# Head sums of an RWKV-7 block as single full-precision products, and third buffers for three evacuation tiles

## The chip, the cores and the metric

The kernel runs on one core of one Trainium2 chip. The metric is the device time of one execution in microseconds (us); the kernel before took 1866.65 us, the median of three runs (1861.1 to 1870.76 us). PE is TensorE, DVE is VectorE, ACT is ScalarE, POOL is GpSimd, SP is SyncE, which only issues DMAs here.

## What is computed

One layer of a decoder with two parallel branches, for a prompt of 1024 tokens and 8 samples of 8 tokens (1088 columns in all). Branch A is sliding-window attention; branch B is RWKV-7 time mixing, with 16 heads of 64 channels. The change touches branch B alone. What bears on it, from the reference:

```
kk = k * k_k.reshape(B_HEADS, HEAD_DIM)
kk = kk / jnp.maximum(jnp.sqrt(jnp.sum(kk * kk, axis=-1, keepdims=True)), 1e-12)
...
y, wkv_T = wkv_scan(r, decay, k, v, -kk, kk * a, wkv0)
mean = jnp.mean(y, axis=-1, keepdims=True)
var = jnp.mean(jnp.square(y - mean), axis=-1, keepdims=True)
y = (y - mean) * lax.rsqrt(var + GN_EPS) * lnx_g + lnx_b
y = y + jnp.sum(r * k * r_k, axis=-1, keepdims=True) * v
```

There are four sums over a head's 64 channels: the norm of the key (kk * kk), the mean of y, its variance, and the bonus (r * k * r_k).

## The kernel before

Channels lie on the 128 partitions (two heads to a tile), tokens on the free axis. The 8 tiles of two heads are worked through in pairs (p = 0 to 3), and each in four quarters of 256 tokens (the fourth has 320, the samples with it): 16 steps s of two tiles each, so 32 quarters in all.

**Dense projections.** All weight products are `d` tiles: operands are split into a high and a low part of type float32r (`whi`, `wlo`, `hhi`, `hlo`), and three products of 8 instructions each make one chunk of 364 or 360 columns (`mm3`, L183). Each chunk is evacuated by ACT, POOL and DVE. For a token-shifted projection (`shift_tile`, L391), ACT writes `pad` and `zz` (L404 to L406), POOL adds them (L407), and the result goes to DRAM. The tiles `pad` and `zz` have two buffers each, which gates (`gevac`), other projections (`spill`), `lora` and the raw low-rank weights (L655) share.

**The recurrence.** For each step s, `prefetch` (L643) loads a quarter from DRAM and squares the key into `kkn` on ACT (L663); `quarter` (L670) makes decay and key norm; `scores`, `invert` and `merge` build a small inverse, in which DVE runs 15 dependent pairs of tiny operations (L854, L856); `chain` (L921) carries the state through four chunks of 64 tokens, each with three rounds of PE product and DVE copy (`xs` L954, `vsu` L959, `vsu` L970); `post` (L1022) does the normalisation of y.

**The four sums.** Each is a product with a constant 128x128 matrix: `bone` (ones within a head) or `cen` (identity less the mean). The operand is first split by `split` (L232): ACT copies it to a float32r tile `shi` (L235), DVE subtracts that from the original into `slo` (L236); each of the two tags has one buffer in a pool. `sum2` (L239) then adds the two products in PSUM. The results are named `kn` (key norm, L694), `bo` (bonus, L745), `gc` (centring, L1029) and `gv` (variance, L1035); the halves are `shik`/`slok`, `shib`/`slob`, `shic`/`sloc`, `shiv`/`slov`. With 32 quarters there are 128 sums.

**The order.** On PE the order of the recurrence and the dense stream is written by the program: generators yield at points where they must wait, and `drive` (L142) picks the next by a planned clock. That clock is advanced by `mm` (L111) by a cost of each product:

```
self.clk += 0.024 if rhs.shape[0] == 32 else max(n / 2190, 0.085) if rhs.dtype == F32R else n / 1200 if transpose else max(n / 580, 0.066)
```

The other engines' orders are made by the framework's scheduler, by priorities. All engines take their instructions strictly in order. After the recurrence come the attention (`attention`) and the last projections (`final`), which the change does not touch.

Of the kernel before, what the change touches and what calls it, by code (L numbers as in the profile page):

```python
# [81 lines left out]
class Prog:  # L82
# [148 lines left out]

    def split(self, pool, src, n, nm):  # L232
        hi = pool.tile([P, 320], F32R, tag="shi", name=f"shi{nm}", bufs=1)[:, :n]
        lo = pool.tile([P, 320], F32R, tag="slo", name=f"slo{nm}", bufs=1)[:, :n]
        self.nc.scalar.activation(hi, src, AF.Copy)  # L235
        self.nc.vector.tensor_tensor(lo, src, hi.bitcast(F32), ALU.subtract)  # L236
        return hi, lo

    def sum2(self, ps, w, parts):  # L239

        self.mm(ps, w, parts[0], start=True, stop=False)
        self.mm(ps, w, parts[1], start=False, stop=True)


# [37 lines left out]
    def start(self, xp, w0):  # L282
# [7 lines left out]
        self.rco = ep.tile([P, NCONST - C_MI], F32, name="rco")  # L290
        self.bone = ep.tile([P, P], F32R, name="bone")
        self.cen = ep.tile([P, P], F32R, name="cen")
        bc = xp.tile([P, 2, P], F32, name="bc")
        for t, i in ((self.con, self.I["con"][:, :C_MI]), (prm, self.I["par"]), (self.rco, self.I["con"][:, C_MI:]),
# [89 lines left out]
        go(tk)  # L384
        nc.gpsimd.tensor_copy(self.bone, bc[:, 0, :])
        nc.gpsimd.tensor_copy(self.cen, bc[:, 1, :])
        nc.gpsimd.dma_start(self.O["ck"], self.I["ckn"][:, NS:, :])
# [3 lines left out]
    def shift_tile(self, idx, ti, out):  # L391

        nc, ep = self.nc, self.ep
        mu, om = self.par(Q_MU + ti), self.prd[:, ti:ti + 1]
        prev = [None]

        def evac(c0, c1, ps):
            m = min(c1, SEQ) - c0
            pad = ep.tile([P, 369], F32, tag="pad", name=f"pad{ti}_{c0}", bufs=2)
            z = ep.tile([P, 364], F32, tag="zz", name=f"zz{ti}_{c0}", bufs=2)  # L400
            if prev[0] is None:
                nc.vector.memset(pad[:, 0:1], 0.0)
# [28 lines left out]
    def gate(self, g):  # L431
        nc, ep = self.nc, self.ep

        def gevac(c0, c1, ps):
            t = ep.tile([P, 364], F32, tag="zz", name=f"gz{g}_{c0}", bufs=2)[:, :c1 - c0]
            x = ep.tile([P, 369], F32, tag="pad", name=f"gx{g}_{c0}", bufs=2)[:, :c1 - c0]
            nc.scalar.activation(x, ps, AF.Copy)
            self.sig_neg(t, t, x, -1.0, 0.0)
            nc.gpsimd.tensor_tensor(t, x, t, ALU.mult)
            nc.gpsimd.dma_start(self.d_g[g][:, c0:c1], t)  # L440
            self.mark(f"g{g}_{c0}")
        yield from self.dense(T_RKVG + 4 * g + 3, self.hhi, self.hlo, gevac)

    def spill(self, idx, dst, kind="copy", scale=1.0):
# [3 lines left out]
        def evac(c0, c1, ps):  # L448
            t = ep.tile([P, 364], F32, tag="zz", name=f"sp{idx}_{c0}", bufs=2)[:, :c1 - c0]
            if kind == "copy":  # L450
                nc.scalar.activation(t, ps, AF.Copy, scale=scale)
            else:
                x = ps
                if kind == "silu":
                    x = ep.tile([P, 369], F32, tag="pad", name=f"sx{idx}_{c0}", bufs=2)[:, :c1 - c0]
                    nc.scalar.activation(x, ps, AF.Copy)
# [186 lines left out]
    def prefetch(self, g, q):  # L643
# [10 lines left out]
        else:  # L654
            raw = ep.tile([P, 364], F32, tag="zz", name=f"w2r{nm}", bufs=2)[:, :2 * P]  # L655
            nc.sync.dma_start(raw, self.I["lora"][:, g].rearrange("p j c -> p (j c)"))
# [4 lines left out]
        nc.sync.dma_start(zk[:, :n], self.d_z[g][1][:, 256 * q:256 * q + n])  # L661
        kkn = ep.tile([P, 320], F32, tag="kkn", name=f"kkn_{nm}", bufs=2)
        nc.scalar.activation(kkn[:, :n], zk[:, :n], AF.Square, scale=self.par(Q_KK + g))  # L663
        parts = self.split(ep, kkn[:, :n], n, f"k{nm}")
        zr = ep.tile([P, 320], F32, tag="zr", name=f"zr_{nm}", bufs=2)
        nc.sync.dma_start(zr[:, :n], self.d_z[g][0][:, 256 * q:256 * q + n])
        self.mark(f"pf{nm}")
        return w2, zk, kkn, parts, zr

    def quarter(self, g, q, gi, f, pre):  # L670
# [8 lines left out]

        w2, zk, kkn, parts, zr = pre  # L680
        yield f"pf{g}_{q}", WD + 4.0 * gi, "m"
# [11 lines left out]
        pk = self.ps("a", f"kn{nm}", 2)  # L693
        self.sum2(pk[:, :n], self.bone, parts)  # L694
        if gi == 0:
# [43 lines left out]
    def bonus(self, g, q, S):  # L739
        nc, ep = self.nc, self.ep  # L740
        n, a0, zk, zv = 320 if q == 3 else 256, 256 * q, S["zk"], S["zv"]
        parts = self.split(ep, zk[:, :n], n, f"b{g}_{q}")
        yield None, WB + 2.0 * (g % 2), "m"
        ps = self.ps("m", f"bo{g}_{q}")
        self.sum2(ps[:, :n], self.bone, parts)  # L745
        nc.vector.tensor_tensor(zk[:, :n].rearrange("p (c s) -> p c s", s=64), ps[:, :n].rearrange("p (c s) -> p c s", s=64), zv[:, :n // 64, 0, :], ALU.mult)
        nc.sync.dma_start(self.d_b[g][:, a0:a0 + n], zk[:, :n])
# [274 lines left out]
    def post(self, g, nm, t, w, y):  # L1022
        nc, cp = self.nc, self.pp
        y = y[:, :w]
        rs = cp.tile([P, 320], F32, tag="gb", name=f"gn{nm}", bufs=2)[:, :w]
        parts = self.split(cp, y, w, f"c{nm}")
        yield None, WP, "t"
        ps = self.ps("t", f"gc{nm}")[:, :w]
        self.sum2(ps, self.cen, parts)  # L1029
        nc.scalar.activation(rs, ps, AF.Square)  # L1030
        nc.vector.tensor_copy(y, ps)
        parts = self.split(cp, rs, w, f"v{nm}")
        yield None, 1.0 + WP, "t"
# [565 lines left out]
```

## Time and profile before

| what | value |
|---|---|
| median of three runs | 1866.65 us |
| the profiled execution's own time | 1864.38 us |
| its span | 1862.6 us |
| instructions in the span | 37492 |
| mean granted TensorE clock | 0.949 of full |
| DVE busy | 1139.5 us, 61% of the span |
| ACT busy | 932.9 us, 50% |
| POOL busy | 618.0 us, 33% |

The rows further down come from several views of that one execution. A group row gives a line, an engine, an operation, the tile written and the tiles read, a shape and a count; then the total busy time in us and the mean of one in ns; after the second bar, the engine's idle time just before these instructions and what ended it. A row of the waits says which instruction waited for which: the total in us, the number of waits, the longest. A row of the timeline gives the start in us, the length in us, the engine and what it did. In the row of stretches, each engine's busy time stands with its number of instructions, then the granted share of TensorE's clock, the share of time in which DMA engines were busy, and GB/s. PEld is the loading of weights on TensorE. A full-precision float32 product shows as two MATMUL rows, a float32r one as one.

### The profile page before, as it was taken

Reading aid. Unit: us, or ns where it says so; the run is one execution under the profiler, and the core shown is the slowest. Engines: PE = TensorE matmul, PEld = TensorE weight load, DVE = VectorE, ACT = ScalarE, POOL = GpSimd, SP = SyncE. Lnnn points to the kernel's source line nnn. Section 1 sums busy time; section 2 is a strip of 40 time slices with the busy share of each in tenths; the row PEclk is TensorE's granted clock in tenths of the full one; section 3 lists DMA queues with packets and bytes.
Section 4 is the critical chain, followed back from the end, with each engine's and each line's share of the span. In section 5 each row is a group of like instructions: output and inputs, shape, how many; then the busy total and the mean of one; then the engine's idle time right before and its main releaser. Section 6 shows DMA issues by size and latency. Waiting matters only on the chain. (4 is left out here: it accounts for less than half of the span.)

```text
span 1862.6 us, 37492 instructions
## 1 busy us (share of the span) xinstructions
PE 1686.4 (91%) x13792; PEld 1584.5 (85%) x13792; DVE 1139.5 (61%) x3224; ACT 932.9 (50%) x2353; POOL 618.0 (33%) x872
## 2 busy tenths in 40 slices
PE   5899889888888989889888899999999999999997
PEld 4799888887787878778888888899999899899997
DVE  5323667866777676787676578642366776544443
ACT  5444555444445556555545565434466765432233
POOL 5466444444442653445463343344200000000000
PEclk8899999898898999999999899999999999999999
DMA  4234433333333334334333343223612344364531
GB/s 159 103 126 128 110 97 95 99 97 88 90 97 103 103 93 115 99 101 112 91 105 97 102 136 89 73 90 101 196 60 66 122 130 149 114 221 133 181 109 60
DMA packets 233687, 206.90 MB, mean 111 GB/s; under 512 B 135904, under 2 KB 202608, under 8 KB 233472
## 3 DMA queue, kind: packets, MB, share of 16 engines
q1 hardware_dynamic: 214624, 149.33, 28.0%
q0 software_dynamic: 18880, 55.17, 9.3%
q8 instruction: 109, 1.79, 0.4%
q14 instruction: 74, 0.61, 0.1%
HBM read 140.42 MB, written 65.98 MB: 111 GB/s over the span
## 5 line engine op out<-in xcount | busy, mean ns | idle before, releaser
L110 PE MATMUL d<-hhi,whi 128*128 128x364 f32 (+1 forms) x1656 | 585.7, 354 | 28.6 <-ACT zz L406 9.5
L110 PE MATMUL d<-hlo,whi 128*128 128x364 f32 (+1 forms) x1656 | 568.2, 343 | 11.0 <-DVE hlo L352 8.3
L110 PEld LDWEIGHTS d<-hhi,whi 128*128 128x128 f32 x1656 | 329.6, 199 | 36.5 <-ACT zz L406 10.7
L110 PEld LDWEIGHTS d<-hlo,whi 128*128 128x128 f32 x1656 | 329.5, 199 | 21.0 <-DVE hlo L352 13.0
L110 PE MATMUL d<-hhi,wlo 128*128 128x364 f32 (+1 forms) x1656 | 340.7, 343 | 0.0
L110 PEld LDWEIGHTS d<-hhi,wlo 128*128 128x128 f32 x1656 | 286.5, 196 | 3.4 <-issue 2.4
L171 POOL TENSOR_TENSOR wlo<-wraw,whi 128x1024 fp32r<-128x1024 f32 x56 | 134.3, 2398 | 144.8 <-PE d L110 53.4
L170 ACT ACTIVATE whi<-wraw 128x1024 fp32r<-128x1024 f32 x90 | 94.9, 1055 | 72.8 <-PE d L110 50.7
L1434 POOL TENSOR_TENSOR xr<-xr,frs 128x256 f32<-128x256 f32 x2 | 1.8, 932 | 344.7 <-ACT frs L1431 344.7
L407 POOL TENSOR_TENSOR zz<-zz,pad 128x364 f32<-128x364 f32 (+1 forms) x75 | 71.9, 959 | 116.0 <-ACT pad L404 54.6
L946 POOL TENSOR_TENSOR sp<-vsu,pc 64x128 f32<-64x128 f32 x128 | 57.2, 446 | 125.1 <-DVE vsu L970 115.8
L970 DVE SCALAR_TENSOR_TENSOR vsu<-c,pc,sp 64x64 f32<-64x64 f32 x240 | 67.9, 283 | 41.1 <-PE c L110 37.9
L854 DVE TENSOR_TENSOR Tt<-TM,TR 128x30 f32<-128x30 f32 (+3 forms) x300 | 81.8, 273 | 17.6 <-DMA TM<-s 8.5
L856 DVE TENSOR_TENSOR TR<-TR,Tt 128x30 f32<-128x30 f32 (+3 forms) x300 | 87.3, 291 | 7.1
L1173 ACT ACTIVATE sc<-sc,st 128x256 f32<-128x256 f32 (+1 forms) x128 | 61.8, 484 | 24.5 <-DVE st L1169 24.4
L405 ACT ACTIVATE pad<-d,prm 128x364 f32<-128x364 f32 (+1 forms) x75 | 40.6, 541 | 57.4 <-PE d L110 57.1
L110 PE MATMUL c<-vsu,kbt 128*128 128x128 f32 x256 | 43.1, 292 | 26.0 <-DVE vsu L959 25.9
L1084 POOL TENSOR_TENSOR ylo<-ys,yhi 128x364 fp32r<-128x364 f32 (+1 forms) x6 | 6.5, 1078 | 178.0 <-ACT yhi L1083 178.0
L110 PE MATMUL d<-yhi,whi 128*128 128x364 f32 (+1 forms) x192 | 64.7, 337 | 0.6 <-DVE mb L1354 0.6
L110 PEld LDWEIGHTS c<-vsu,kbt 128*128 128x128 f32 x256 | 36.6, 196 | 33.4 <-DVE vsu L959 32.6
L110 PE MATMUL d<-ol,whi 128*128 128x364 f32 (+1 forms) x192 | 63.1, 329 | 1.5 <-DVE ol L230 1.5
L110 PE MATMUL d<-oh,whi 128*128 128x364 f32 (+1 forms) x192 | 63.3, 330 | 1.2 <-ACT oh L229 1.2
(362 smaller groups left out, 3883.5 us busy)
## 6 DMA issues: line engine op xcount, KB each, us to landing
wraw<-in_w POOLq DMA_DIRECT2D x56, 512.0 KB, 4.2
wraw<-in_w SPq DMA_DIRECT2D x37, 512.0 KB
d_z<-zz POOLq DMA_DIRECT2D x48, 182.0 KB, 2.4
zv<-d_z SPq DMA_DIRECT2D x48, 128.0 KB
w<-d_c SPq DMA_DIRECT2D x24, 256.0 KB
d_m<-sp SPq DMA_DIRECT2D x32, 182.0 KB
stageo<-d_o SPq DMA_DIRECT2D x8, 544.0 KB
d_z<-zz POOLq DMA_DIRECT2D x24, 180.0 KB, 3.8
```

The costliest lines, as they stand in the source:

```text
L110: self.nc.tensor.matmul(out, lhsT=lhsT, rhs=rhs, **kw)
L170: nc.scalar.activation(hi, raw, AF.Copy)
L171: (nc.vector if self.dve_lo else nc.gpsimd).tensor_tensor(lo, raw, hi.bitcast(F32), ALU.subtract)
L405: nc.scalar.activation(pad[:, 1:1 + m], ps[:, :m], AF.Copy, scale=mu)
L407: nc.gpsimd.tensor_tensor(z[:, :m], z[:, :m], pad[:, 0:m], ALU.add)
L854: nc.vector.tensor_tensor(tv, M[:np_, s:s + 1, s + 1:16].to_broadcast([np_, cc, w]), R[:np_, 0:cc, s:s + 1].to_broadcast([np_, cc, w]), AL ...
L856: nc.vector.tensor_tensor(R[:np_, 0:cc, s + 1:16], R[:np_, 0:cc, s + 1:16], tv, ALU.add)
L946: nc.gpsimd.tensor_tensor(sp[h], vsu[h, c, :, h], pc[h, c].unsqueeze(2).to_broadcast([64, 2, HD]), ALU.mult)
L970: nc.vector.scalar_tensor_tensor(dst, pn[h, i, h], pc[h, c, i:i + 1], sp[h, i], ALU.mult, ALU.add)
L1084: (self.nc.gpsimd if kt % 4 == 3 else self.nc.vector).tensor_tensor(lo, t, hi.bitcast(F32), ALU.subtract)
L1173: nc.scalar.activation(sc[k], sc[k], AF.Exp, bias=st[:, 0, k:k + 1], accum_out=st[:, 1, k:k + 1])
L1434: en.tensor_tensor(xt[:, dt, :n], xt[:, dt, :n], rst[:, :n], ALU.mult)
```

## The change

The four sums become one product each, of float32 operands, with no split of the operand: `split` and `sum2` are gone, and the constants are read as float32 straight from the tile that was loaded, so that the two POOL casts go too. The tags `pad`, `zz` and `kkn` get a third buffer each. Lines after the removed functions move up by 12 to 19, so that L1031 of before is L1013 after.

```
-    def split(self, pool, src, n, nm):
-        hi = pool.tile([P, 320], F32R, tag="shi", name=f"shi{nm}", bufs=1)[:, :n]
-        lo = pool.tile([P, 320], F32R, tag="slo", name=f"slo{nm}", bufs=1)[:, :n]
-        self.nc.scalar.activation(hi, src, AF.Copy)
-        self.nc.vector.tensor_tensor(lo, src, hi.bitcast(F32), ALU.subtract)
-        return hi, lo
-
-    def sum2(self, ps, w, parts):
-
-        self.mm(ps, w, parts[0], start=True, stop=False)
-        self.mm(ps, w, parts[1], start=False, stop=True)
...
-        self.bone = ep.tile([P, P], F32R, name="bone")
-        self.cen = ep.tile([P, P], F32R, name="cen")
-        bc = xp.tile([P, 2, P], F32, name="bc")
+        bc = ep.tile([P, 2, P], F32, name="bc")
+        self.bone, self.cen = bc[:, 0, :], bc[:, 1, :]
...
-        nc.gpsimd.tensor_copy(self.bone, bc[:, 0, :])
-        nc.gpsimd.tensor_copy(self.cen, bc[:, 1, :])
...
-            pad = ep.tile([P, 369], F32, tag="pad", name=f"pad{ti}_{c0}", bufs=2)
-            z = ep.tile([P, 364], F32, tag="zz", name=f"zz{ti}_{c0}", bufs=2)
+            pad = ep.tile([P, 369], F32, tag="pad", name=f"pad{ti}_{c0}", bufs=3)
+            z = ep.tile([P, 364], F32, tag="zz", name=f"zz{ti}_{c0}", bufs=3)
...
-        kkn = ep.tile([P, 320], F32, tag="kkn", name=f"kkn_{nm}", bufs=2)
+        kkn = ep.tile([P, 320], F32, tag="kkn", name=f"kkn_{nm}", bufs=3)
         nc.scalar.activation(kkn[:, :n], zk[:, :n], AF.Square, scale=self.par(Q_KK + g))
-        parts = self.split(ep, kkn[:, :n], n, f"k{nm}")
...
-        self.sum2(pk[:, :n], self.bone, parts)
+        self.mm(pk[:, :n], self.bone, kkn[:, :n], start=True, stop=True)
...
-        parts = self.split(ep, zk[:, :n], n, f"b{g}_{q}")
         yield None, WB + 2.0 * (g % 2), "m"
         ps = self.ps("m", f"bo{g}_{q}")
-        self.sum2(ps[:, :n], self.bone, parts)
+        self.mm(ps[:, :n], self.bone, zk[:, :n], start=True, stop=True)
...
-        parts = self.split(cp, y, w, f"c{nm}")
         yield None, WP, "t"
         ps = self.ps("t", f"gc{nm}")[:, :w]
-        self.sum2(ps, self.cen, parts)
+        self.mm(ps, self.cen, y, start=True, stop=True)
         nc.scalar.activation(rs, ps, AF.Square)
         nc.vector.tensor_copy(y, ps)
-        parts = self.split(cp, rs, w, f"v{nm}")
         yield None, 1.0 + WP, "t"
         p2 = self.ps("t", f"gv{nm}")[:, :w]
-        self.sum2(p2, self.bone, parts)
+        self.mm(p2, self.bone, rs, start=True, stop=True)
```

Every other use of the tags `pad` and `zz` gets `bufs=3` in the same way.

Since the planned clock charges the new products otherwise, the order moves. On PE, where the first centring (`gc0_0`) stands beside the fourth key norm (`kn0_3`) and the chain's step 1, chunk 0 (`c0_10`, `y0_10`; `lo` are the low-rank products, `A` scores, `d` dense). Before:

```order
L110 MATMUL c0_10_3218<-vsu0_1_2174,X2_743 128x128
L110 MATMUL c0_10_3218<-vsu0_1_2174,X3_744 128x128
L110 MATMUL y0_10_3221<-X2_743,vsu0_1_2174 128x128
L110 MATMUL y0_10_3221<-X3_744,vsu0_1_2174 128x128
L110 MATMUL lo0_30_3230<-zl0_3_3135,w2_0_3_3137 128x320 x2
L110 MATMUL lo0_31_3231<-zl0_3_3135,w2_0_3_3137 128x320 x2
L110 MATMUL kn0_3_3242<-shik0_3_3143,bone_172 128x320
L110 MATMUL kn0_3_3242<-slok0_3_3144,bone_172 128x320
L110 MATMUL gc0_0_3275<-shic0_0_3154,cen_173 128x256
L110 MATMUL gc0_0_3275<-sloc0_0_3155,cen_173 128x256
L110 MATMUL d15_1_3284<-hhi364_149,whi15_2851 128x364
```

and now:

```order
L110 MATMUL A0_201_3124<-X0_737,KB0_2_2446 128x128
L110 MATMUL A0_200_3123<-X0_737,KB0_2_2446 128x128
L110 MATMUL A0_201_3124<-X0_737,KB0_2_2446 128x128
L110 MATMUL lo0_30_3139<-zl0_3_3036,w2_0_3_3038 128x320 x2
L110 MATMUL lo0_31_3140<-zl0_3_3036,w2_0_3_3038 128x320 x2
L110 MATMUL kn0_3_3151<-kkn_0_3_3042,bc_172 128x320
L110 MATMUL c0_10_3111<-xs0_10_3112,ti_735 128x64 x2
L110 MATMUL gc0_0_3183<-ysb0_00_2549,bc_172 128x256
L110 MATMUL d15_0_3096<-hhi0_144,whi15_2793 128x364
L110 MATMUL d15_0_3096<-hlo0_145,whi15_2793 128x364
```

Each pair is one product now, the chain's next product (`c0_10` from `xs0_10`) has come in between the two sums, and the dense tile beside it is chunk 0 of tile 15 where it was chunk 1: the chain stands earlier in the dense stream.

On DVE, the same place, from the chain's update of `vsu` on. Before:

```order
L970 SCALAR_TENSOR_TENSOR vsu0_1_2174<-c0_03_2960,pc0_0_1664,sp0_03_2962 64x64 x4
L236 TENSOR_TENSOR sloc0_0_3155<-ysb0_00_2610,shic0_0_3154 128x256
L411 TENSOR_SCALAR pad19_728_3497<-shp_169,prm_139 128x8
L808 TENSOR_TENSOR am0_2_3121<-A0_200_3200,rco_171 128x4x64
L954 COPY xs0_10_3219<-c0_10_3218 64x128 x2
L809 TENSOR_TENSOR X0_741<-A0_200_3200,rco_171 64x4x64
L808 TENSOR_TENSOR am0_2_3121<-A0_201_3201,rco_171 128x4x64
L809 TENSOR_TENSOR X0_741<-A0_201_3201,rco_171 64x4x64
L712 TENSOR_SCALAR kkn_0_3_3141<-kn0_3_3242 128x320
L236 TENSOR_TENSOR slok1_3_3252<-kkn_1_3_3249,shik1_3_3251 128x320
L1031 COPY ysb0_00_2610<-gc0_0_3275 128x256
L236 TENSOR_TENSOR slov0_0_3281<-gn0_0_3153,shiv0_0_3280 128x256
```

and now:

```order
L953 SCALAR_TENSOR_TENSOR vsu0_1_2131<-c0_03_2852,pc0_0_1641,sp0_03_2854 64x64 x4
L937 COPY xs0_10_3112<-c0_10_3111 64x128 x2
L791 TENSOR_TENSOR am0_2_3022<-A0_200_3123,rco_171 128x4x64
L792 TENSOR_TENSOR X0_737<-A0_200_3123,rco_171 64x4x64
L791 TENSOR_TENSOR am0_2_3022<-A0_201_3124,rco_171 128x4x64
L792 TENSOR_TENSOR X0_737<-A0_201_3124,rco_171 64x4x64
L691 SCALAR_TENSOR_TENSOR sg_0_3_3165<-rco_171,sg_0_3_3165 128x332
L696 TENSOR_SCALAR kkn_0_3_3042<-kn0_3_3151 128x320
L942 COPY vsu0_1_2131<-c0_10_3111 64x2x64 x2
L702 TENSOR_SCALAR e1_0_3_3179<-e1_0_3_3146,prm_139,prd_140 128x320
L1013 COPY ysb0_00_2549<-gc0_0_3183 128x256
```

Three subtractions (L236) and the write of `pad` (L411) are gone from between the chain's copies; the copy `xs0_10`, which the chain's next product needs, now follows the update of `vsu` at once.

## Rows read from the trace of the kernel before

**Rows 1.** The page, busy time of each engine over the span.
```profile
PE 1686.4 (91%) x13792; PEld 1584.5 (85%) x13792; DVE 1139.5 (61%) x3224; ACT 932.9 (50%) x2353; POOL 618.0 (33%) x872
```
**Rows 2.** Stretches: start:end and length, PE, PEld, DVE, ACT, POOL busy, clock, DMA.
```profile
200.00:1250.00 1050.00, 923.88 (x8834) 863.77 (x8832) 735.93 (x2159) 548.51 (x1421) 464.77 (x684) 0.93 0.36 100
1250.00:1340.00 90.00, 87.53 (x560) 86.09 (x560) 27.95 (x54) 44.11 (x87) 34.82 (x38) 0.98 0.47 145
1340.00:1660.00 320.00, 316.56 (x2362) 293.58 (x2359) 205.80 (x710) 182.18 (x509) 6.47 (x6) 0.99 0.39 124
```
**Rows 3.** Waits of PE between 200 and 1250 us.
```profile
PE c L110 <- DVE vsu L959: 25.9, 19, 4.4
PE c L110 <- DVE xs L954: 15.5, 9, 3.2
PE lo L110 <- DVE X L809: 11.4, 7, 3.1
...
PE d L110 <- ACT zz L406: 5.8, 2, 3.3
```
**Rows 4.** Chain of waits by line, between 1035 and 1298 us (first), 1074 and 1082 us (second).
```profile
by line: PE d L110 38.0%; PE c L110 5.6%; DVE Tt L854 4.8%; issue 4.4%; DVE TR L856 4.2%; PE y L110 3.2%; PE A L110 2.0%; DMA sin<-in_wkv 1.4%; DMA d_b<-zk 1.4%; PE ss_d L110 1.3%; DVE xs L954 1.3%; DVE vsu L959 1.2%; PE ss_a L110 1.2%; DMA
...
by line: DVE Tt L854 23.4%; DVE TR L856 19.9%; issue 11.3%; PE d L110 8.2%; DVE sg L707 7.6%; DVE vsu L959 7.3%; DVE vsu L970 6.0%; PE c L110 5.7%; DVE kkn L712 5.3%; DVE slok L236 4.2%; DVE xs L954 4.1%; DVEq L854 0.6%
```
**Rows 5.** Timeline of PE at full clock: a pair of 256, one of 320, a float32 product.
```profile
605.47 0.28 PE L110 MATMUL gv<-shiv,bone 128*128 128x256 f32 x1
605.59 0.28 PE L110 MATMUL gv<-slov,bone 128*128 128x256 f32 x1
605.71 0.60 PE L110 MATMUL c<-vsu,X 128*128 128x128 f32 x4
...
609.68 0.31 PE L110 MATMUL bo<-shib,bone 128*128 128x320 f32 x1
...
609.98 0.82 PE L110 MATMUL d<-hhi,wlo 128*128 128x360 f32 x4
...
1269.01 1.02 PE L110 MATMUL ss_d<-ve,kbs 128*128 128x512 f32 x2
1269.87 0.55 PE L110 MATMUL c<-xs,ti 128*128 128x64 f32 x4
1270.23 0.41 PE L110 MATMUL d<-hhi,whi 128*128 128x364 f32 x1
1270.48 0.33 PE L110 MATMUL d<-hlo,whi 128*128 128x364 f32 x1
1270.65 0.33 PE L110 MATMUL d<-hhi,whi 128*128 128x364 f32 x1
```
**Rows 6.** Groups of instructions: the split on DVE and ACT, a product that reads it.
```profile
L236 DVE TENSOR_TENSOR slok<-kkn,shik 128x256 fp32r<-128x256 f32 (+1 forms) x32 | 22.4, 699 | 9.7 <-ACT shik L235 9.3
L236 DVE TENSOR_TENSOR slov<-gn,shiv 128x256 fp32r<-128x256 f32 (+1 forms) x32 | 18.1, 567 | 0.7 <-ACT shiv L235 0.2
L236 DVE TENSOR_TENSOR sloc<-ysb,shic 128x256 fp32r<-128x256 f32 (+1 forms) x32 | 17.0, 530 | 27.4 <-ACT shic L235 27.2
L236 DVE TENSOR_TENSOR slob<-zk,shib 128x256 fp32r<-128x256 f32 (+1 forms) x32 | 15.9, 498 | 2.0 <-ACT shib L235 1.8
...
L235 ACT ACTIVATE shic<-ysb 128x256 fp32r<-128x256 f32 (+1 forms) x32 | 13.7, 428 | 5.5 <-PE gv L110 5.1
L235 ACT ACTIVATE shib<-zk 128x256 fp32r<-128x256 f32 (+1 forms) x32 | 13.7, 428 | 36.4 <-DVE zk L735 21.3 <-PE bo L110 8.2 <-DVE TR L856 5.3
...
L110 PE MATMUL gc<-shic,cen 128*128 128x256 f32 (+1 forms) x32 | 11.5, 358 | 0.0
```
**Rows 7.** Groups of instructions that take a buffer of `pad` or `kkn`.
```profile
L411 DVE TENSOR_SCALAR pad<-shp,prm 128x8 f32<-128x8 f32 x25 | 6.6, 266 | 60.5 <-POOL zz L407 60.4
L663 ACT ACTIVATE kkn<-zk,prm 128x256 f32<-128x256 f32 (+1 forms) x32 | 16.7, 520 | 59.3 <-DMA zk<-d_z 31.8 <-DVE X L762 27.4
```
**Rows 8.** Waits of DVE between 60 and 200 us.
```profile
DVE pad L411 <- POOL zz L407: 42.3, 5, 17.9
```

More of the change, by code (lines that the diff above doesn't have):

```diff
@@ L434, in gevac @@
         def gevac(c0, c1, ps):
-            t = ep.tile([P, 364], F32, tag="zz", name=f"gz{g}_{c0}", bufs=2)[:, :c1 - c0]
-            x = ep.tile([P, 369], F32, tag="pad", name=f"gx{g}_{c0}", bufs=2)[:, :c1 - c0]
+            t = ep.tile([P, 364], F32, tag="zz", name=f"gz{g}_{c0}", bufs=3)[:, :c1 - c0]
+            x = ep.tile([P, 369], F32, tag="pad", name=f"gx{g}_{c0}", bufs=3)[:, :c1 - c0]
             nc.scalar.activation(x, ps, AF.Copy)
@@ L448, in evac @@
         def evac(c0, c1, ps):
-            t = ep.tile([P, 364], F32, tag="zz", name=f"sp{idx}_{c0}", bufs=2)[:, :c1 - c0]
+            t = ep.tile([P, 364], F32, tag="zz", name=f"sp{idx}_{c0}", bufs=3)[:, :c1 - c0]
             if kind == "copy":
@@ L454, in evac @@
                 if kind == "silu":
-                    x = ep.tile([P, 369], F32, tag="pad", name=f"sx{idx}_{c0}", bufs=2)[:, :c1 - c0]
+                    x = ep.tile([P, 369], F32, tag="pad", name=f"sx{idx}_{c0}", bufs=3)[:, :c1 - c0]
                     nc.scalar.activation(x, ps, AF.Copy)
@@ L481, in lora @@
         n = c1 - c0
-        t = ep.tile([P, 364], F32, tag="zz", name=f"tl{c0}", bufs=2)
+        t = ep.tile([P, 364], F32, tag="zz", name=f"tl{c0}", bufs=3)
         self.sig_neg(t[0:64, :n], t[0:64, :n], z[0:64, :n], -2.0, 0.0)
@@ L654, in prefetch @@
         else:
-            raw = ep.tile([P, 364], F32, tag="zz", name=f"w2r{nm}", bufs=2)[:, :2 * P]
+            raw = ep.tile([P, 364], F32, tag="zz", name=f"w2r{nm}", bufs=3)[:, :2 * P]
             nc.sync.dma_start(raw, self.I["lora"][:, g].rearrange("p j c -> p (j c)"))
@@ L667, in prefetch @@
         self.mark(f"pf{nm}")
-        return w2, zk, kkn, parts, zr
+        return w2, zk, kkn, zr
     def quarter(self, g, q, gi, f, pre):
@@ L678, in E @@
             return ep.tile([P, w], F32, tag=tag, name=f"{tag}_{nm}", bufs=bufs)
-        w2, zk, kkn, parts, zr = pre
+        w2, zk, kkn, zr = pre
         yield f"pf{g}_{q}", WD + 4.0 * gi, "m"
```

## The prediction

> **What bounds the kernel now.** I read the busy shares first, then the stretches, then PE's waits, then the chain of waits. PE is busy for 91% of the span [rows 1], which looks like a kernel bound by its products. The stretches tell it apart: from 1250 to 1660 us PE is busy for 97 to 99% at a clock of 0.98 to 0.99, and the change touches almost nothing there. From 200 to 1250 us, where nearly all the recurrence and its sums lie, PE is busy for 923.9 of 1050 us, and its granted clock is 0.93 [rows 2], a mixture of stretches at 2.4 and at 1.2 GHz. So 126 us go in waits, and the low clock takes 7% of 1050, 74 us, more: 200 us in which PE does not work at full speed. That pool is where this change can win, since it only adds work to PE.
>
> Whom PE waits for stands in its waits [rows 3]: mostly DVE, with the chain's copies `vsu` (25.9 us) and `xs` (15.5), then `X` (11.4). DVE is busy for 735.9 of the 1050 us, 70%; an urgent copy stands in line behind whatever was put ahead of it. The chain of waits shows the same: between 1035 and 1298 us the named PE lines carry 51% of it (38.0, 5.6, 3.2, 2.0, 1.3 and 1.2), and for whole stretches, as from 1074 to 1082 us, it runs almost on DVE alone, with a split's subtraction `slok` in it for 4.2% of 8 us, 0.34 us [rows 4].
>
> **What is added: PE time.** At full clock a pair of float32r products of 256 columns takes 605.47 to 605.71, 0.24 us; a pair of 320 takes 609.68 to 609.98, 0.30 us. The trace has no full-precision sum of 256, but it has one of 512 columns of the same shape of weights: 1269.01 to 1269.87, 0.86 us [rows 5]. In proportion that is 0.43 us for 256 and 0.54 for 320. There are 96 sums of 256 and 32 of 320: 96 x 0.19 = 18.2 us and 32 x 0.24 = 7.7 us, together 25.9 us. A dense product that follows a float32 one is followed by the next after 0.25 us (1270.23 to 1270.48) where 0.17 is usual (1270.48 to 1270.65): 0.08 us for each return to float32r. In the new order, 64 of the 128 sums stand between two float32r products, so this adds 64 x 0.08 = 5.1 us. At the stretch's clock of 0.93 the 31 us become **34 us** of PE time. Bounds: 25.9 us if the return costs nothing and the clock is full; (25.9 + 128 x 0.08) / 0.93 = 39 us if each sum pays it.
>
> Not all of that is time. A product that is added ahead of a wait shortens the wait by as much. Where the chain of waits runs over another engine, PE's extra is covered; PE's named share of that chain is 51%, a little more with the lines that are not named. I take 55%: of 34 us, 19 come through and **15 are covered**. If the cover went, because DVE is no longer late, all 34 would show, but then the waits would have gone too.
>
> **What is removed: places in the queues of DVE and ACT.** DVE loses 128 subtractions, 22.4 + 18.1 + 17.0 + 15.9 = 73.4 us, and 39.8 us in which it stood before them waiting for ACT's half (27.4 of it before `sloc`): 113 us of its queue. ACT loses 128 copies; the shown groups of 32 have 13.7 us each, so some 55 us for four, and waits of 36.4 us before `shib` and 5.5 before `shic` [rows 6]. What stood behind moves up; next in line is then mostly the same copy of the chain, which must still wait for its own product. How much of PE's 200 us this gives back the trace cannot show, so I bound it. From below: nothing, if the chain's copies were late for other reasons (the 15 dependent pairs of L854 and L856 alone are 43% of the chain from 1074 to 1082 us [rows 4]). From above: a queue's wait goes roughly as busy share over free share, an estimate; DVE goes from 736 busy of 1050 to 736 less some 70, from 0.70 to 0.63, and the ratio from 2.35 to 1.73, 26% less; 26% of 200 us is 52 us. I take two thirds of the upper bound, **33 us**, nearer the top since DVE's lost waits of 40 us are not in it, and ACT's relief is not either, and not at the top since the rows of PE's waits are led by copies whose product has only just ended.
>
> **Third buffers.** DVE stands 60.5 us before L411 for POOL's add, whose tile the buffer still is [rows 7]; but 42.3 us of that lie before 200 us [rows 8], where DVE has little to do and PE hardly waits for it. ACT stands 27.4 us before L663 until DVE has read the `kkn` of two quarters before [rows 7]. It then still waits for the load of `zk` (31.8 us in the same row), which the third buffer doesn't bring sooner. PE's own waits that end with the evacuation of a dense chunk are 5.8 us after `zz` [rows 3]. I take **3 us** off; bounds 0 and 8. The two POOL casts that go run once, beside dense work on an engine busy for 33% [rows 1]: nothing, and without that cover under 1 us, an estimate from the 266 ns of L411, which is as small.
>
> **The order.** The planned clock charges a float32 product of 256 with 0.44 us where two float32r ones were 0.23, so about as the trace does; the chain keeps its planned distances, and with more time between its steps there are fewer dense products between them. I count nothing for that, with bounds of 10 us either way from chance changes of who meets whom: single waits of PE are up to 4.4 us long [rows 3].
>
> **The sum.** Against the profiled execution of 1864.4 us: + 34 - 15 - 33 - 3 = -17, so 1847.4. The median of the runs is 2.3 us above the profiled one, so the forecast for it is **1850 us** (0.9% faster). A measurement of this kernel can tell some 0.5%, 9.3 us, from no change.
>
> **The rivals.**
> *Slower: PE is the bound and pays.* The mechanism is the doubled PE time of the sums at the places where PE runs dense work with DVE in time. For it speaks 91% busy [rows 1], and that the split was no visible wait where it was longest: before `gc` PE never stood idle [rows 6]. Relief of 0 with the cover kept gives 1866.65 + 34 - 15 = 1886 us; without cover, 1901. It decides from the point where cover and relief together are under 25 us (34 less 9.3). Against it stand 126 us of waits. By the same view the weight loads cover 863.8 of 1050 us on PE, 82%, more than DVE's 70% [rows 2]. The Trainium skill (Perfetto Trace Analysis, Identifying the Most-Contended Engine) says to work on the engine with most contention and judges TensorE by the busy share of its weight loads; by that rule TensorE comes first here, and trading DVE time for TensorE time would lose, at 1901 us. The chain of waits, with half of it off PE, speaks against that rule here. Chance 22%.
>
> *No change: the two sides meet.* If DVE's relief is only what lies directly on the chain of waits (0.34 us in 8 us on the DVE stretch, and none on the PE stretches), it is 4.2% of the 45% or so off PE, 1.9% of 1050, 20 us, and that less 19 for PE is nothing: 1866 us. For it speaks that PE's waits come at the chain, whose rhythm is set by latency. Chance 28%.
>
> *Faster by much: the head-of-line stalls were it.* If ACT's 27.4 us and DVE's 18.2 us (60.5 less 42.3) of buffer waits were passed on to PE whole, another 43 us would go (45.6 less the 3 taken): 1807 us. Against it: only 5.8 us of PE's waits end at `zz`. Chance 5%.
>
> That the change doesn't do what it says can be left out: the order shows one product a sum and no L235 or L236.
>
> **How the numbers follow.** Forecast 45%, slower 22%, no change 28%, much faster 5%. Faster by over 0.5%: 45 + 5 = 50%; within 0.5%: 28%; slower: 22%. The range goes from the upper bound of relief and buffers (1866.65 + 34 - 15 - 52 - 8 = 1826) to no relief at all (1886). Outside lie the much faster case and the slower one without cover, and part of the mishaps of order, under 20% together. Within the forecast's own case it is 1835 to 1857 us.
>
> **What would show it.** Right: `kn`, `bo`, `gc`, `gv` with two rows a sum and about 0.43 us from start to start; no L235 or L236; DVE busy some 70 us less; PE busy up by about 30 us, or by less if the clock rises; between 200 and 1250 us a clock over 0.93, and the waits of `c` for `vsu` and `xs` well under 41 us. Wrong: the same waits of `c` with a longer span (relief is worth nothing); waits before the sums themselves, on `kkn`, `ysb` or `gn`; a dense product that waits 0.2 us or more after each sum; or the waits of `kkn` moved whole onto the load of `zk`.

## The result

The changed kernel took 1843.69 us (median of four runs, 1838.97 to 1846.85) beside 1865.24 us of the kernel before on the same chip: a ratio of 0.9884, with an interval of 0.985 to 0.9919. The forecast was 1850 us, 0.9% faster. The profiled execution took 1845.48 us with a span of 1843.7 us.

The page of the kernel after, busy time of each engine:

```profile
PE 1692.9 (92%) x13792; PEld 1581.6 (86%) x13792; DVE 1062.9 (58%) x3096; ACT 886.6 (48%) x2225; POOL 615.6 (33%) x870
```

Against [rows 1], DVE has lost 76.6 us and 128 instructions, ACT 46.3 us and 128; PE has 6.5 us more. The stretches of after that answer to [rows 2]:

```profile
200.00:1250.00 1050.00, 943.73 (x8988) 873.50 (x8987) 675.17 (x2065) 513.94 (x1324) 474.39 (x697) 0.96 0.37 100
1250.00:1340.00 90.00, 88.85 (x544) 87.51 (x543) 28.31 (x64) 44.73 (x90) 22.55 (x24) 1.00 0.50 154
1340.00:1660.00 320.00, 315.91 (x2319) 292.48 (x2318) 202.27 (x683) 173.67 (x481) 6.61 (x6) 0.98 0.41 126
```

In the 1050 us of the recurrence PE now does 8988 products where it did 8834, at a granted clock of 0.96 where it was 0.93. The two later stretches are as they were. PE's waits from 200 to 1250 us, after:

```profile
PE c L110 <- DVE vsu L942: 28.4, 17, 4.0
PE c L110 <- DVE vsu L953: 10.3, 9, 2.2
...
PE c L110 <- DVE xs L937: 7.2, 8, 2.3
...
PE d L110 <- ACT zz L391: 2.5, 2, 2.1
```

The chain's waits for `vsu` (L942, before L959) and `xs` were 25.9 + 15.5 = 41.4 us [rows 3] and are 28.4 + 7.2 = 35.6. That is less, but not the fall on which the forecast rested. Two more views of after say where to look. The groups of the sums and of the buffers' takers:

```profile
L110 PE MATMUL kn<-kkn,bc 128*128 128x256 f32 (+1 forms) x64 | 22.5, 435 | 8.8 <-ACT e L674 6.3 <-DVE X L792 1.9 <-ACT sg L684 0.6
L110 PE MATMUL bo<-zk,bc 128*128 128x256 f32 (+1 forms) x64 | 22.0, 427 | 10.2 <-DVE TR L839 5.4 <-DVE sx L976 3.0 <-DVE ras L993 1.8
L110 PE MATMUL gv<-gn,bc 128*128 128x256 f32 (+1 forms) x64 | 20.7, 406 | 4.1 <-DVE tc L876 3.7 <-DVE ysb L1013 0.4
L110 PE MATMUL gc<-ysb,bc 128*128 128x256 f32 (+1 forms) x64 | 20.2, 397 | 0.0
...
L648 ACT ACTIVATE kkn<-zk,prm 128x256 f32<-128x256 f32 (+1 forms) x32 | 16.7, 521 | 75.9 <-DMA zk<-d_z 60.7 <-DVE X L745 15.2
...
L396 DVE TENSOR_SCALAR pad<-shp,prm 128x8 f32<-128x8 f32 x25 | 6.3, 252 | 47.4 <-POOL zz L399 36.0 <-POOL gz L424 11.1
```

Each sum stands as two rows (x64 for 32 sums), and no split is left. ACT stands before `kkn` (L648, before L663) for longer than it did, 75.9 us against 59.3 [rows 7], and now for the load of `zk`. DVE stands before `pad` (L396, before L411) for 47.4 us against 60.5 [rows 7].

The page's numbers give the account that the rest of this text uses: PE does the same products in before, after and most of the experiments, so a change of its span is one of busy time (the clock, or longer products) or of idle time (span less busy). From before to after: busy 1686.4 to 1692.9, +6.5; idle 176.2 to 150.8, -25.4. Each profile is one execution, and the two parts are not equally firm. Three experiments below run at one speed (ratios 0.9991, 0.9999 and 0.9991): their idle time is 159.8, 160.7 and 160.9 us, but their busy time 1701.9, 1688.0 and 1693.6, as the clock of the one execution happens to be. So a difference of some 14 us in busy time can be chance.

### The profile page after: what moved, and what is told of

Read it like the earlier page. It is cut to its first block, busy times and chain, and to the rows that moved or that the text cites. A ratio compares the mean times of both kernels' runs of the same rounds, so it can differ in the third digit from the quotient of the medians.

```text
span 1843.7 us, 37106 instructions
## 1 busy us (share of the span) xinstructions
PE 1692.9 (92%) x13792; PEld 1581.6 (86%) x13792; DVE 1062.9 (58%) x3096; ACT 886.6 (48%) x2225; POOL 615.6 (33%) x870
## 3 DMA queue, kind: packets, MB, share of 16 engines
q1 hardware_dynamic: 214624, 149.33, 28.4%
## 4 chain that ended last, share of the span: by engine, by line
PE 58%; DVE 17%; DMA 9%; issue 5%; POOL 4%; ACT 4%; SPq 1%; DVEq 0%; POOLq 0%; ACTq 0%
PE d L110 35%; PE wo L110 5%; DVE Tt L837 3%; DVE TR L839 3%; PE c L110 3%; PE s L110 2%; PE A L110 2%; PE o L110 2%; PE y L110 2%; DMA wraw<-in_w 1%; PE pt L108 1%; DMA dinv<-s 1%; DVE KB L715 1%; DMA TM<-s 1%; DVE vsu L953 1%
## 5 line engine op out<-in xcount | busy, mean ns | idle before, releaser
L110 PE MATMUL d<-hlo,whi 128*128 128x364 f32 (+1 forms) x1656 | 560.6, 339 | 10.9 <-DVE hlo L339 7.7
L110 PEld LDWEIGHTS d<-hlo,whi 128*128 128x128 f32 x1656 | 323.3, 195 | 21.8 <-DVE hlo L339 12.1
L110 PEld LDWEIGHTS d<-hhi,whi 128*128 128x128 f32 x1656 | 323.1, 195 | 21.0 <-ACT whi L170 6.1
L839 DVE TENSOR_TENSOR TR<-TR,Tt 128x30 f32<-128x30 f32 (+3 forms) x300 | 79.0, 263 | 7.7
L1154 ACT ACTIVATE sc<-sc,st 128x256 f32<-128x256 f32 (+1 forms) x128 | 61.8, 484 | 25.9 <-DVE st L1150 25.7
L110 PE MATMUL c<-vsu,kbt 128*128 128x128 f32 x256 | 42.7, 291 | 28.4 <-DVE vsu L942 28.4
L715 DVE TENSOR_TENSOR KB<-e,sg 64x256 f32<-64x256 f32 x128 | 65.1, 519 | 1.4
```

The costliest lines, as they stand in the source:

```text
L110: self.nc.tensor.matmul(out, lhsT=lhsT, rhs=rhs, **kw)
L715: nc.vector.tensor_tensor(KB[hr, :4, j, :], self.v64(t)[hr], self.d64(Pi, 1)[hr], ALU.mult)
L839: nc.vector.tensor_tensor(R[:np_, 0:cc, s + 1:16], R[:np_, 0:cc, s + 1:16], tv, ALU.add)
L1154: nc.scalar.activation(sc[k], sc[k], AF.Exp, bias=st[:, 0, k:k + 1], accum_out=st[:, 1, k:k + 1])
```

## The experiments

The two theories after the result: the relief of DVE and ACT paid for the longer products (the forecast's), or the gain is that of the buffers. Lines of the experiments are those of after, a few lower down where something was added.

### The sums alone, the buffers alone

**Sums alone.** The change without its third buffers:

```
-            pad = ep.tile([P, 369], F32, tag="pad", name=f"pad{ti}_{c0}", bufs=3)
+            pad = ep.tile([P, 369], F32, tag="pad", name=f"pad{ti}_{c0}", bufs=2)
```

and the same for every use of `pad`, `zz` and `kkn`.

> The changed kernel with two buffers again for pad, zz and kkn: the single products alone. Relief theory (shorter DVE and ACT queues outweigh the longer products; third buffers worth 3 us): 1847 us, between 1840 and 1856. Buffer theory (the third buffers made the gain): no gain, or the bare cost of the products, 1866 to 1885 us.

Measured: 1860.39 us, ratio 0.9991 [0.997, 1.0013]. The single products with all their relief are worth nothing.

**Third buffers of `pad` and `zz` alone** (with single products, `kkn` back to two):

> The changed kernel with kkn back at two buffers: single products, and third buffers for pad and zz alone. Evacuation theory (the gain is the evacuation of shifted chunks, which no longer waits for POOL's add or its store): as the changed kernel, ratio 0.985 to 0.992. Key-norm theory (the gain is ACT no longer held at the key's square): as the sums alone, 0.996 to 1.003.

1837.48 us, ratio 0.9881 [0.9857, 0.9906]: as much as the whole change gains.

**The third `kkn` alone** (`pad` and `zz` back to two):

> The changed kernel with pad and zz back at two buffers: single products and the third kkn buffer alone. Evacuation theory: 0.996 to 1.003. Key-norm theory: 0.985 to 0.992. If both buffers give part, both runs lie near 0.994.

1858.24 us, ratio 0.9999 [0.9978, 1.002]: nothing. Its group row says why:

```profile
L648 ACT ACTIVATE kkn<-zk,prm 128x256 f32<-128x256 f32 (+1 forms) x32 | 16.7, 520 | 67.5 <-DMA zk<-d_z 52.1 <-DVE X L745 15.2
```

Beside the row of the sums alone,

```profile
L648 ACT ACTIVATE kkn<-zk,prm 128x256 f32<-128x256 f32 (+1 forms) x32 | 16.7, 522 | 74.4 <-DVE X L745 37.0 <-DMA zk<-d_z 30.7 <-DVE e L869 4.8
```

the 22 us that ACT no longer waits for DVE it waits for the load of `zk`, which has two buffers as before.

**`pad` alone and `zz` alone:**

> Single products and a third buffer for pad alone (pad holds DVE at L411 and L402 of before, and ACT at L404). If DVE's and ACT's waits for the add of a shifted chunk are what counted: 0.985 to 0.993. If zz: 0.996 to 1.003.

1849.42 us, ratio 0.9947 [0.9929, 0.9964].

> Single products and a third buffer for zz alone (zz is held until its store to DRAM has landed, and POOL issues that store). If what counted is ACT waiting for the store: 0.985 to 0.993. If pad: 0.996 to 1.003.

1851.41 us, ratio 0.9953 [0.9931, 0.9975]. Beside 0.9991 each gives some 0.4%, the two together 1.1%; with intervals of 0.2% either way they add, as far as that tells.

**The new order alone:** the kernel before, split and pairs kept, with the planned clock charged as in the change, so that PE's order is planned as after's:

```
     def sum2(self, ps, w, parts):
+        c = self.clk
         self.mm(ps, w, parts[0], start=True, stop=False)
         self.mm(ps, w, parts[1], start=False, stop=True)
+        self.clk = c + parts[0].shape[1] / 580
```

> The kernel before with its splits and pairs, but the planned clock charged for each sum as in the changed kernel: the new order alone. Relief theory: no gain, 1860 to 1875 us. Order theory: most of the gain, 1840 to 1852 us.

1861.76 us, ratio 0.9998 [0.9976, 1.002]: nothing, as the forecast had it.

### Why the sums come to nothing

**The products without the relief:** the sums alone, with ACT's copy and DVE's subtraction put back, but unread, so that PE waits for neither:

```
+    def dead(self, pool, src, n, nm):
+        hi = pool.tile([P, 320], F32R, tag="shi", name=f"shi{nm}", bufs=1)[:, :n]
+        self.nc.scalar.activation(hi, src, AF.Copy)
+        lo = pool.tile([P, 320], F32R, tag="slo", name=f"slo{nm}", bufs=1)[:, :n]
+        self.nc.vector.tensor_tensor(lo, src, hi.bitcast(F32), ALU.subtract)
```

> As e1_sums, but the split's ACT copy and DVE subtraction are put back as work that nobody reads: the products' cost without the relief. Relief theory: slower than before by the 19 us of PE time that come through, 1885 us (range 1876 to 1900). Order theory (the new planned order made the gain, the queues are beside the point): as fast as e1_sums, 1845 to 1850 us.

1883.0 us, ratio 1.0114 [1.0083, 1.0144]: the longer products cost 21 us (0.0114 x 1863.15). The page of this kernel, and that of the sums alone:

```profile
PE 1704.2 (91%) x13792; PEld 1589.7 (85%) x13792; DVE 1123.8 (60%) x3224; ACT 933.1 (50%) x2353; POOL 621.7 (33%) x870
```

```profile
PE 1701.9 (91%) x13792; PEld 1590.0 (85%) x13792; DVE 1066.4 (57%) x3096; ACT 889.2 (48%) x2225; POOL 614.3 (33%) x870
```

With spans of 1879.1 and 1861.7 us, PE is idle for 174.9 and 159.8 us; before it was 176.2. So in these profiles the longer products add 17.8 us of busy time and take 1.3 us of idle time away; then taking 57.4 us of work from DVE and 43.9 from ACT takes 15.1 us of idle time away and 2.3 of busy time. The 15.1 us are clear of the spread of idle time above; the 17.8 can be off by chance.

**The relief without the longer products:** the split is gone, but each sum is two float32r products, of an operand that its producer writes as float32r. Two buffers for `pad`, `zz` and `kkn`. Some operands get tiles of their own, among them the centred `y` (`yc`, one buffer).

```
+    def sum1(self, ps, w, x):
+        self.mm(ps, w, x, start=True, stop=False)
+        self.mm(ps, w, x, start=False, stop=True)
...
-        kkn = ep.tile([P, 320], F32, tag="kkn", name=f"kkn_{nm}", bufs=2)
+        kq = ep.tile([P, 320], F32R, tag="kkn", name=f"kkn_{nm}", bufs=2)
...
-        self.mm(pk[:, :n], self.bone, kkn[:, :n], start=True, stop=True)
+        self.sum1(pk[:, :n], self.bone, kq[:, :n])
```

> No split, but two float32r products as before, on operands written as float32r (both products take the same rounded operand with half the weights, so the low part is left out): the relief without the products' cost, at the old planned order. Relief theory: 33 us under before or a little more, 1815 to 1838 us. Order theory: no gain, 1860 to 1870 us.

1854.39 us, ratio 0.9949 [0.9925, 0.9973].

These four make a square: short products with the split's work 1, without it 0.9949; long products with it 1.0114, without it 0.9991. By that the relief is worth 0.5% beside short products and 1.2% beside long ones, and the long products cost 1.1% in full queues and 0.4% in relieved ones. But the relief with short products brings waits of its own. PE's waits from 200 to 1250 us in that kernel:

```profile
PE gv L110 <- DVE yc L1024: 9.8, 3, 4.7
PE q_2a L110 <- DVE yc L1024: 2.4, 1, 2.4
```

The other kernels have no tile `yc`, and over the span DVE stands 27.1 us in four waits before it for its store to DRAM. These 12.2 us of PE's waits are about the 13 us by which the two figures of the relief differ. So it is not shown that cost and relief do not add; the relief beside long products, 1.2%, is the firmer figure.

**Whose relief:** the sums alone with an unread subtraction on DVE, none on ACT.

```
+    def dead(self, pool, src, n, nm):
+        lo = pool.tile([P, 320], F32R, tag="slo", name=f"slo{nm}", bufs=1)[:, :n]
+        self.nc.vector.tensor_tensor(lo, src, src, ALU.subtract)
```

> Single products, two buffers, with an unread subtraction put back on DVE alone (ACT keeps its relief). If the relief is DVE's, as the forecast had it, this gives about 1.011 as with both; if it is ACT's, about 0.999; shared, between.

1875.15 us, ratio 1.0072 [1.0043, 1.0102]. Between 0.9991 and 1.0114: DVE's work is worth some 0.8%, 15 us, ACT's the remaining 0.4%, 8 us. The intervals of 1.0072 and 1.0114 overlap, so ACT's share is the less certain one. Nor is DVE's share its work alone: here too it stands before the subtraction for ACT, 40.5 us before `slok` until `kkn` is written (with both, 30.5 us for ACT's copy).

### What the third buffers take away

**The raw weights apart.** In the trace of the sums alone, ACT waits for the load of `w2r`, which shares the tag `zz`, and PE once stands 2.8 us behind that. One theory was that `zz`'s share of the gain is this load.

```
-            raw = ep.tile([P, 364], F32, tag="zz", name=f"w2r{nm}", bufs=2)[:, :2 * P]
+            raw = ep.tile([P, 2 * P], F32, tag="w2r", name=f"w2r{nm}", bufs=1)
```

> Single products, pad, zz and kkn with two buffers, but the raw low-rank weights (tile w2r) have a buffer of their own instead of sharing zz. If the gain of the third zz buffer is the late load of w2r, this gives the same as the third zz buffer alone: ratio about 0.995 to the kernel before, and the waits of ACT for the DMA of w2r fall from 21.2 us to under 10. If the gain lies in the evacuation of the dense chunks (zz between ACT and POOL), it stays at 0.999.

1860.17 us, ratio 0.9991 [0.9971, 1.0012]. The waits of ACT for that load are gone from 200 to 1250 us, where they were 13.9 us, and the time has not moved: this theory fell. What else shares `zz`, above all the evacuation of dense chunks, is left; which of its waits the third buffer shortens was not followed.

**The place where it can be seen.** Waits of DVE for a buffer of `pad` from 200 to 1250 us, in the sums alone:

```profile
DVE pad L396 <- POOL zz L392: 21.9, 7, 11.8
DVE pad L387 <- POOL zz L392: 10.9, 5, 3.4
```

and after:

```profile
DVE pad L396 <- POOL zz L399: 9.0, 1, 9.0
```

So 32.8 us in 12 waits have become 9.0 in one. This is the buffer of `pad`. A third buffer of `zz` alone leaves these waits as they were, 21.8 and 9.3 us, and gains as much; its share of the account is open. The longest of the 12 shows what such a wait does. DVE in the sums alone, around 930 us (start, length, what it did, and in brackets the idle time before it and what ended that):

```profile
927.62 0.42 DVE L1013 COPY ysb<-gc 128x256 f32<-128x256 f32 x1
929.03 0.42 DVE L869 TENSOR_TENSOR e<-q_3a,moff 128x256 f32<-128x256 f32 x1 [0.98 <-PE q_3a L110]
941.30 0.23 DVE L396 TENSOR_SCALAR pad<-shp,prm 128x8 f32<-128x8 f32 x1 [11.85 <-POOL zz L392]
941.44 0.42 DVE L876 TENSOR_TENSOR tc<-q_3b,dinv 128x256 f32<-128x256 f32 x1
```

For 11.85 us DVE stands before an instruction of 0.23 us, eight columns of `pad`. Behind it waits `tc`, whose product `q_3b` PE had done at 932.5. POOL over the same time:

```profile
932.64 2.02 POOL L858 DMA_DIRECT2D dinv<-s  x4 [6.97 <-DMA s<-TR]
934.68 2.36 POOL L171 TENSOR_TENSOR wlo<-wraw,whi 128x1024 fp32r<-128x1024 f32 x1
936.97 0.53 POOL L894 COPY tis<-dinv 32x64 f32<-32x64 f32 x2
937.58 0.80 POOL L392 TENSOR_TENSOR zz<-zz,pad 128x296 f32<-128x296 f32 x1
938.34 0.31 POOL L399 TENSOR_TENSOR zz<-zz,pad 128x64 f32<-128x64 f32 x1
...
940.33 0.94 POOL L392 TENSOR_TENSOR zz<-zz,pad 128x364 f32<-128x364 f32 x1
```

POOL is late with the adds that read `pad` because it stood 6.97 us for a transfer and then split a weight tile (`wlo`). With two buffers the third chunk's `pad` needs the buffer of the same tile's first chunk, so the add at 940.33; with three it needs that of the last tile's third chunk, the add (L399) that ended some 2.6 us sooner. PE meanwhile:

```profile
934.56 0.82 PE L110 MATMUL d<-hhi,wlo 128*128 128x364 f32 x4
941.92 1.22 PE L110 MATMUL gv<-gn,bc 128*128 128x256 f32 x2 [6.53 <-DVE tc L876]
942.58 1.77 PE L110 MATMUL d<-hhi,wlo 128*128 128x364 f32 x4
944.15 0.50 PE L110 MATMUL d<-hhi,whi 128*128 128x360 f32 x1
944.45 0.50 PE L110 MATMUL d<-hlo,whi 128*128 128x360 f32 x1
```

`gv` goes into the PSUM tag `t`, of one buffer, which `tc` still has to read; PE stands for 6.53 us, and the wait is put down to `tc`, not to `pad`. Then the dense products come every 0.30 us where 0.17 is usual [rows 5]. The stretches (PE busy first, the clock behind POOL):

```profile
926.00:934.00 8.00, 8.00 (x167) 7.46 (x167) 2.19 (x11) 2.31 (x7) 1.36 (x3) 1.00 0.24 61
935.50:941.90 6.40, 0.00 (x0) 0.00 (x0) 0.56 (x3) 0.20 (x1) 5.79 (x11) 0.76 0.36 116
941.90:945.80 3.90, 3.88 (x12) 3.71 (x13) 0.44 (x1) 2.05 (x4) 2.66 (x7) 0.51 0.34 107
945.90:950.00 4.10, 4.10 (x68) 3.61 (x68) 0.91 (x3) 2.17 (x5) 1.51 (x3) 1.00 0.13 34
```

Before the wait the granted clock was 1.00 (2.4 GHz), after it 0.51 (1.2 GHz) for 3.9 us, then 1.00 again: the wait costs 6.5 us and about half of 3.9, 1.9 us, on top. After the change the same place reads

```profile
918.89 0.82 PE L110 MATMUL d<-hhi,wlo 128*128 128x364 f32 x4
923.42 1.22 PE L110 MATMUL gv<-gn,bc 128*128 128x256 f32 x2 [3.70 <-DVE tc L876]
```

a wait of 3.70 us. This one place is 2.8 us of idle time. The clock is not given back there: DVE still stands 9.0 us before `pad`, and after PE's wait the granted clock is low for even longer.

```profile
923.40:928.10 4.70, 4.68 (x14) 4.18 (x14) 0.45 (x1) 1.46 (x3) 4.07 (x10) 0.50 0.55 193
```

Over the whole span, PE's idle time is 159.8 to 160.9 us in the three kernels of one speed that have two buffers for `pad` and `zz`; with three it is 150.8 (after) and 144.9 (after, `kkn` at two). So 9 to 16 of the 20 us gained are waits of PE. Whether the rest is the clock, the profiles cannot tell: between the runs of the sums alone the mean clock goes from 0.953 to 0.965. Its mean over all runs is 0.958 there and 0.962 after, but 0.963 with the raw weights apart, a kernel that is no faster than the sums alone. The other places were not followed one by one as this one was.

**Do the buffers need the relief?** The unread copies and subtractions again, of at most 256 columns and into one tile so that it fits, with third buffers for `pad` and `zz`:

```
+        n = min(n, 256)
+        hi = pool.tile([P, 256], F32R, tag="shi", name=f"shi{nm}", bufs=1)
+        self.nc.scalar.activation(hi, src[:, :n], AF.Copy)
+        self.nc.vector.tensor_tensor(hi, src[:, :n], hi.bitcast(F32), ALU.subtract)
```

> Single products with the unread ACT copy and DVE subtraction put back (on 256 columns, written to one tile), and third buffers for pad and zz. With two buffers the like kernel was at 1.0114. If the buffers are worth the same 1.1% when the queues of DVE and ACT are as full as before, this comes to about 1.000. If the buffers only pay once the queues are relieved, it stays near 1.011; if they pay more in full queues, it falls below 0.997.

1867.57 us, ratio 1.0037 [1.0012, 1.0061], beside 1.0114 without the buffers: 0.8% in full queues where 1.1% in relieved ones, a difference that lies within the intervals. They pay in both, and here PE's idle time falls from 174.9 to 161.4 us while its busy time stays (1704.2 and 1704.5): waits alone. The buffers alone on the kernel before do not fit into its memory, so what they would have given there was not tried. For the buffers, the use of the single products was the room that the split's tiles left.

### A version that is faster

With third buffers for `pad` and `zz`, `kkn` at two, and two of the four sums (`kn`, `gv`) as one float32r product:

```
-        self.mm(pk[:, :n], self.bone, kkn[:, :n], start=True, stop=True)
+        self.mm(pk[:, :n], self.bone, kq[:, :n], start=True, stop=True)
...
-        self.mm(p2, self.bone, rs, start=True, stop=True)
+        self.mm(p2, self.bone, rr, start=True, stop=True)
```

with `bone` a float32r tile for these two, and `kq` and `rr` the float32r tiles that hold `kkn` and `gn`.

> Candidate: third buffers for pad and zz, kkn with two, and the key norm and the variance as one float32r product each, of an operand that is written as float32r (their squares lose the low part, so those two sums are of lower precision); centring and bonus stay full precision. If the two halves add, the buffers' 1.2% and about half of the product cost (20 us for 128 sums, so 10 us or 0.5%): ratio about 0.983. If the cost was only the float32 products' in the chain, which bonus and centring keep, 0.988.

1829.92 us, ratio 0.9834 [0.9802, 0.9866].

```profile
PE 1665.7 (91%) x13728; PEld 1566.4 (86%) x13728; DVE 1075.5 (59%) x3096; ACT 886.3 (49%) x2225; POOL 617.8 (34%) x871
```

PE has 27 us less work than after (1692.9), and the time is 0.5% lower. That interval and after's (0.985 to 0.9919) overlap by 0.0016 at the edge, so that it is faster than after is likely rather than shown. Of the two expectations it is the first, 0.983; the second, 0.988, lies outside the interval. It is a trade against the precision of two sums, which the change does not make.

## Why the prediction was right, and where it was wrong

The sign and the size were right: -17 us forecast against the profiled execution, -18.9 measured between the two profiled ones (1845.48 less 1864.38). The split into terms was not, and that the total came out is luck: the products, their cover and the relief were to give -14 us and gave next to nothing (0.9991), the buffers were to give -3 and gave -20, and the two errors cancel.

**Third buffers: the step that failed.** It took 3 us off with bounds of 0 and 8; measured are 0.9991 to 0.9884, 1.07% or 20 us, all of it from `pad` and `zz`. Two arguments carried the 3. The first, that 42.3 of L411's 60.5 us lie where DVE has little to do [rows 8], is true, but it took the 18.2 us that remain as if they stayed the same. From 200 to 1250 us DVE's waits for a buffer of `pad` are, before and then with the new order alone:

```profile
DVE pad L411 <- POOL zz L407: 18.1, 10, 2.6
DVE pad L402 <- POOL zz L407: 2.8, 3, 1.6
...
DVE pad L413 <- POOL zz L409: 19.2, 8, 9.1
DVE pad L404 <- POOL zz L409: 7.6, 4, 3.1
```

That is 20.9 and 26.8 us; with the long products and the split's work it is 29.7, in the sums alone 32.8, and with the relief alone in the old order 29.8. So the order makes these waits longer as well as the relief does (the longest, 2.6 us before, is 9.1), though by itself it cost no time (0.9998). The second argument, that only 5.8 us of PE's waits end at `zz` [rows 3], reads the wrong row: what waits behind `pad` on DVE is an instruction that PE needs, and PE's wait then bears that one's name, as `tc` did at 942 us. This is shown at that one place, for 2.8 us; how the other 17 come about, and all of what `zz` gives, stays open. The rival "faster by much", whose mechanism was just this, was given 5% and 43 us; the measured size is half of that, and of its mechanism DVE's half is borne out by the place that was followed. Its other half, ACT's wait before `kkn`, was worth nothing, as the forecast argued from the load of `zk`. The Trainium skill (Perfetto Trace Analysis, Optimization Strategy) says that a gap repeating on the engine that should be saturated can mean too few buffers for the next tile. Here PE had two such waits before (5.8 us at `zz` [rows 3]); the repeated wait for a buffer stands on DVE, 12 times in the sums alone, and the one that was followed came to PE under another name.

**Relief of the queues.** Taken at 33 us of bounds 0 and 52; measured 23 us beside long products (1.0114 to 0.9991), the case of the change, and 9.5 beside short ones (1 to 0.9949), with some 12 us of new waits in that kernel. Inside its bounds, too high by 10 us. "Nearer the top" was the wrong choice: the wait for `vsu` of L942 did not fall at all (25.9 [rows 3], 30.8 in the sums alone), only that for `xs` did, to 6.2. DVE's share is about two thirds, so leaving ACT's out of the working, but naming it, was a smaller fault.

**PE time of the products.** Forecast 31 us at full clock, of which 19 of 34 come through. Measured 21 us [15, 27]. The working of the length was near. Before, a pair and the four dense products behind it:

```profile
654.01 0.28 PE L110 MATMUL gv<-shiv,bone 128*128 128x256 f32 x1
...
654.25 0.82 PE L110 MATMUL d<-hhi,wlo 128*128 128x360 f32 x4
654.90 0.61 PE L110 MATMUL c<-vsu,X 128*128 128x128 f32 x4
```

and after, a single product and four:

```profile
623.56 0.59 PE L110 MATMUL gc<-ysb,bc 128*128 128x256 f32 x2
623.81 1.01 PE L110 MATMUL d<-hhi,wlo 128*128 128x364 f32 x4
624.66 0.60 PE L110 MATMUL c<-vsu,X 128*128 128x128 f32 x4
```

0.89 us has become 1.10, 0.21 more, return to float32r included, where the forecast had 0.19 and 0.08. Where a float32 product follows the sum, the 0.43 us from start to start that were to be seen stand by themselves, after:

```profile
456.82 0.59 PE L110 MATMUL gv<-gn,bc 128*128 128x256 f32 x2
457.25 0.61 PE L110 MATMUL c<-vsu,kbt 128*128 128x128 f32 x4
```

Where float32r follows, the next row starts 0.25 us after the sum (623.56 to 623.81) and the four dense products then take 0.85 us where they took 0.65. But 1.10 is 0.43 and four times 0.17: the return, taken at 0.08, cost nothing that these rows show, and the 5.1 us for it were too much. The sum over the span agrees roughly: busy time times mean clock goes from 1686.4 x 0.949 = 1600 to 1704.2 x 0.957 = 1631 us without the relief, 31 more, and to between 1624 and 1639 in the ten profiles that have the 128 long products. The cover of 15 us was not found as waits: only 1.3 us of PE's idle time went. The clock of these two profiles, 0.949 and 0.957, would make up for the rest, but over all runs it is 0.952 and 0.954, within the spread. So some 10 us of the work did not show as time, and where they went stays open.

**The order.** Nothing, as forecast: 0.9998.

**The rivals.** "No change: the two sides meet" is what happened to the sums taken alone, 0.9991, on which the forecast spent nearly all its terms; it had 20 us of relief against 19 of cost, measured are 23 and 21. "Slower" would have been right without the relief (1883.0 us; the rival had 1886 for that case). The rule of the Trainium skill (Perfetto Trace Analysis, Identifying the Most-Contended Engine), by which TensorE comes first here, would have given 1901. The trade of DVE time for TensorE time is the sums alone: it neither lost nor won, since the relief took 15.1 us of PE's idle time away. The time then fell through the buffers, with PE's weight loads at 873.50 of 1050 us after, 83% where they were 82%. Where the products alone were lengthened and nothing relieved, 21 us were lost.

**What was to be seen.** DVE 76.6 us less (70 forecast), PE up by 6.5 (30 or less), the clock at 0.96 (over 0.93), as far as one execution tells: right. The waits of `c` "well under 41 us": 35.6, not well under. The wrong sign that was named, `kkn`'s wait moved onto the load of `zk`, did come for the most part: from 31.8 us [rows 7] to 60.7, with 15.2 left to DVE where 27.4 were.

## What to carry to other kernels

A wait for a buffer on an engine that takes its instructions in order, as DVE ran `tc` at 941.44 though its product was done at 932.5, is priced by what is queued behind it, not by the rows of the waits that carry the buffer's name: follow one such wait, as from `pad` to `tc` to `gv`, before giving it a small number. Waits counted in the old kernel do not carry over: when a change moves the order or relieves a queue, expect those on the next resource to change (here 20.9 us before `pad` became 26.8 with the order alone and 32.8 in the sums alone). And where a change does several things, the total can be right with the terms wrong; a kernel for each part shows it, so long as that kernel brings no wait of its own, as the tile `yc` did. Between two single profiles, idle time can be compared more closely than busy time, which moves with the clock of the one execution.

## What the runs showed that was not expected

- A wait of PE can cost twice: after 6.53 us of it the granted clock was 0.51 for 3.9 us, where it had been 1.00 until PE stopped; after, a wait of 3.70 us at the same place was followed by 4.7 us at 0.50.
- The mean clock over all runs is 0.952 to 0.953 in the three kernels with short products and 0.954 to 0.963 in the ten with 128 long ones. Why is not shown, and for the long products without relief, 0.954 from four runs, the difference is within the spread.
- A float32 product of 256 columns took 0.43 us from start to start where a pair of float32r ones took 0.24.
- An instruction of 0.23 us on DVE, which stood 11.85 us for POOL, held PE for 6.53 us.
